# Six heads' share of half of the merge's latent blocks, moved into the attention

## The chip, the cores and the metric

The kernel runs on one core of one Trainium2 chip. The metric is device time in microseconds (us) of one execution; several executions are timed and their median is compared.

## The reference, cut to what matters

One decoder layer: a first feed-forward half-step, two token mixers side by side (softmax "latent" attention with 8 heads, called MLA, and stick-breaking attention with 8 heads, called SB), a gated merge of the two, a second feed-forward half-step and a gated embedding. The change touches the merge alone:

```python
g_mla, g_sb = jnp.split(jax.nn.sigmoid(gates), 2, axis=-1)
merged = g_mla * (o_mla @ w_branch_mla[i]) + g_sb * (o_sb @ w_branch_sb[i])
h = h + merged @ w_out[i]
```

`o_mla` and `o_sb` are 1024 tokens by 512 (8 heads of 64), the branch weights are 512 by 1024, `w_out` is 1024 by 1024. Every product is made of three TensorE products of split numbers (high by high, high by low, low by high), with float32 sums.

## The kernel before, in words

Activations lie channel by token. A weight is loaded by SP's queue into a buffer of the pool `raw` (three buffers of 512 KB, handed out in turn), split by ScalarE (high part) and GpSimd (low part) into a buffer of the pool `d` (six buffers), and used by TensorE (`load_split`, lines 133 to 144). The same three `raw` buffers also carry the gates, outputs and operands of the filling work below. TensorE's order is the order in which the code is written. The order on the other engines and on SP's queue is made by a scheduler from priorities and its own timing model, so it can differ from the written one.

The attention (from line 1097) goes through 48 units, 24 of SB and then 24 of MLA (8 heads with 3 units each). A unit goes in steps: transposes of probabilities, scores of the next unit, products with the values. After each step `fill(ns)` draws *filling work*, which is matmuls of a generator, until the step has taken 2500 ns (SB) or 1600 ns (MLA) of modelled TensorE time. In the SB half the filler is `gates()`. In the MLA half it is `branches_sb()`: for each of eight blocks of 128 channels (`ct`) the product of `o_sb` with the branch weight, times its gate, written to the scratch tensor `msb_d` in HBM. `left[0]` holds the nanoseconds of filler that remain; when it is used up, MLA's steps run without filling, save that the last head's last units empty the generator.

The merge (from line 1288) follows. `merge_up(ct, d)` computes block `ct` of `o_mla` times the branch weight (24 matmuls of 512 columns: two halves of tokens, four pairs of heads, three products), multiplies it by the gate, adds `msb_d` and splits the sum into `hid`. `chunked` (line 267) lays this beside the product with `w_out`: blocks 0, 1 and 2, then `down_chunk` on blocks 0 and 1 (96 matmuls), block 3, block 4, `down_chunk` on 2 and 3, and so on, each with its weight loads. Also at the start of the merge `h` (8 loads of 512 KB from `h_spill`, line 1297) and a gain row (`gbc`, line 209) are loaded.

Of the kernel before, what the change touches and what calls it, by code (L numbers as in the profile page):

```python
# [2 lines left out]

# [8 lines left out]
F32 = mybir.dt.float32  # L12
# [7 lines left out]
P = 128  # L20
# [3 lines left out]
KT = DM // P  # L24
# [22 lines left out]
def hybrid_layer_kernel(  # L47
# [42 lines left out]
    def bank():  # L90
        return pool_of["T"].tile([P, 512], F32, tag="T", name="T")
# [40 lines left out]
    def load_split(parts, n, home=None):  # L132

        raw = rawp.tile([P, 1024], F32, tag="raw", name="raw")
        for c0, src in parts:
            a, b = src.shape[1], src.shape[2]
            nc.sync.dma_start(out=raw[:, c0:c0 + a * b].rearrange("p (a b) -> p a b", a=a), in_=src)
        d = new_d() if home is None else home
        nc.scalar.copy(d[:, HI, :n], raw[:, :n])  # L139
        w = n // pieces[0]  # L140
        for c0 in range(0, n, w):
            c = slice(c0, c0 + w)
            nc.gpsimd.tensor_sub(d[:, LO, c], raw[:, c], d[:, HI, c].bitcast(F32))  # L143
        return d
# [45 lines left out]
    def mm3(ps, lh, ll, rh, rl, start, stop):  # L190
        mm(ps, lh, rh, start, False)
        mm(ps, lh, rl, False, False)
        mm(ps, ll, rh, False, stop)
# [73 lines left out]
    def chunked(h, n, up, wo, scale, ahead, order, after):  # L267

        load, compute = up

        def rows(f0):
            return [w_rows(wo, (f0 + j) * P, 0, 1024) for j in range(2)]

        d0, d1 = load(0), load(1)
        hids = [compute(0, d0), compute(1, d1)]
        for f in range(0, n - 4, 2):
            d0 = load(f + 2)
            dw = rows(f)
            d1 = load(f + 3)
            nxt = [compute(f + 2, d0)]  # L280
            for _ in down_chunk(h, hids, dw, scale):
                pass
            nxt.append(compute(f + 3, d1))
            hids = nxt
        d0, d1 = load(n - 2), load(n - 1)
        dw = rows(n - 4)
        hids.append(compute(n - 2, d0))
        dw += rows(n - 2)
        hids.append(compute(n - 1, d1))
        ahead()  # L290
        for t in down_chunk(h, hids, dw, scale, order):
            after(t)
# [487 lines left out]
    st_p.close()  # L780
    psum_pools(st_p, "2", 2)

    def branch_w(w, ct):
        d = load_split([(0, w[:, ct * P:(ct + 1) * P].rearrange("(k q) c -> q k c", q=P))], 512)
        return d[:, :, :512].rearrange("q l (k c) -> q l k c", k=4)

    def load_row(src, i):
        gt = rawp.tile([P, 1024], F32, tag="raw", name="gt")
        nc.sync.dma_start(out=gt, in_=src[i])
        return gt  # L790

    def branch_mm(ps, d, o, tk):
        for k in range(4):
            mm3(ps, d[:, HI, k], d[:, LO, k], o[HI][:, k, tk], o[LO][:, k, tk], k == 0, k == 3)


    def gates():
# [14 lines left out]
    def branches_sb(first):  # L812

        nxt = first
        for ct in range(KT):
            d = nxt
            if ct + 1 < KT:
                nxt = branch_w(w_branch_sb, ct + 1)
            gt = load_row(gate_d, KT + ct)
            bt = rawp.tile([P, 1024], F32, tag="raw", name="bt")  # L820
            for half in range(2):
                tk = slice(half * 512, (half + 1) * 512)
                ps = bank()
                for k in range(4):
                    mm3(ps, d[:, HI, k], d[:, LO, k], o_t[1][HI][:, k, tk], o_t[1][LO][:, k, tk], k == 0, k == 3)
                    yield
                nc.scalar.copy(bt[:, tk], ps)
                nc.gpsimd.tensor_mul(bt[:, tk], bt[:, tk], gt[:, tk])
            nc.sync.dma_start(out=msb_d[ct], in_=bt)

    filler = [gates()]
# [400 lines left out]
    def start_mla():  # L1232
        first = branch_w(w_branch_sb, 0)
        fill(1e9)
        for b in range(2):
            o_t.append([upool.tile([P, 4, S], F32R, tag="u", name="oT") for _ in range(2)])
        for j in range(4):
            split_o(o_t[1], j, pairs[j], slice(0, S))
        filler[0] = branches_sb(first)
        left[0] = KT * 24 * 216.0  # L1240
# [12 lines left out]
    for n, (m, hd, un) in enumerate(units):  # L1253
        if (m, hd, un) == (1, 0, 0):
            while queue:
                run_av()
            start_mla()
        todo = []
        if n + 1 < len(units):
            m2, hd2, un2 = units[n + 1]  # L1260
            todo = []
            for c in unit_ch[un2]:
                both = (2 * c, 2 * c + 1)
                todo += [(m2, hd2, ix) for ix in ([both] if m2 or c < 2 else [both[:1], both[1:]])]
        if un == 1:
            head_of(m, hd + 1) if hd + 1 < H else head_of(m + 1, 0) if m == 0 else None
        steps = []
        for c in unit_ch[un]:
            steps += av_steps(hd, c, [probs.pop((m, hd, 2 * c + a)) for a in range(2)], head_of(m, hd)[3], m == 1)
        for k, (tr, ac) in enumerate(steps):  # L1270
            t0 = pe["t"]
            take = -(-len(todo) // (len(steps) - k))
            pt = tr()
            for x_ in todo[:take]:
                scores(*x_)
            todo = todo[take:]
            queue.append((pt, ac))
            if len(queue) > 2:
                run_av()
            goal = (2500.0, 1600.0)[m]  # L1280
            if m == 0 or left[0] > 0 or (hd == H - 1 and un > 0):
                fill(t0 + goal - pe["t"])
# [17 lines left out]
    def merge_up(ct, d):  # L1300
        if ct % 2 == 0:
            if ct == 0:
                gmt[0] = [new_d(F32) for _ in range(2)]
            else:
                both = upool.tile([P, 2, 2, S], F32, tag="u", name="gm")
                gmt[0] = [both[:, b] for b in range(2)]
            for b, src in enumerate((gate_d, msb_d)):
                nc.sync.dma_start(out=gmt[0][b], in_=src[ct:ct + 2].rearrange("a q n -> q a n"))
        gt, mt = gmt[0][0][:, ct % 2], gmt[0][1][:, ct % 2]
        pool, bufs = (hid_a, 1) if ct % 4 == 3 else (hid_b, 3)  # L1310
        hid = pool.tile([P, 2, S], F32R, tag="hid", name="hid", bufs=bufs)
        for half in range(2):
            tk = slice(half * 512, (half + 1) * 512)
            ps = bank()
            branch_mm(ps, d, o_t[0], tk)
            m = mp.tile([P, 512], F32, tag="m", name="m", bufs=2)
            nc.vector.tensor_mul(m, ps, gt[:, tk])
            nc.vector.tensor_add(m, m, mt[:, tk])
            split_hidden(hid, tk, m)
        return hid  # L1320
# [12 lines left out]
    def after2(t):  # L1333
# [6 lines left out]
        else:  # L1340
# [3 lines left out]
            left.sums(t - 4, (0,) if t == 4 else (0, 1))  # L1344

    g2 = bcast_row(mp, ffn2_norm, DM)
    chunked(h, KT, (lambda ct: branch_w(w_branch_mla, ct), merge_up), w_out, 1.0, ahead,
            tuple(range(NT)), after2)
    need("a11")
    st.close()  # L1350
# [79 lines left out]
```

## Time and profile before

| what | us |
|---|---|
| median of 3 runs (2368.03 to 2371.63) | 2369.64 |
| the profiled execution's own time | 2370.18 |
| its span on the chip | 2368.3 |
| TensorE (PE) busy in the span | 2294.6 |
| VectorE (DVE) busy | 1525.6 |
| ScalarE (ACT) busy | 959.2 |
| GpSimd (POOL) busy | 847.7 |

The span runs from the first to the last instruction. Times in the rows count from its start. In this execution the filler `branches_sb` ends at about 1425 us, the attention's last value product at 1480 us, and the merge lies from there to about 1621 us.

### The profile page before, as it was taken

Reading aid. Unit: us, or ns where it says so; the run is one execution under the profiler, and the core shown is the slowest. Engines: PE = TensorE matmul, PEld = TensorE weight load, DVE = VectorE, ACT = ScalarE, POOL = GpSimd, SP = SyncE. Lnnn points to the kernel's source line nnn. Section 1 sums busy time; section 2 is a strip of 40 time slices with the busy share of each in tenths; the row PEclk is TensorE's granted clock in tenths of the full one; section 3 lists DMA queues with packets and bytes.
Section 4 is the critical chain, followed back from the end, with each engine's and each line's share of the span. In section 5 each row is a group of like instructions: output and inputs, shape, how many; then the busy total and the mean of one; then the engine's idle time right before and its main releaser. Section 6 shows DMA issues by size and latency. Waiting matters only on the chain.

```text
span 2368.3 us, 30098 instructions
## 1 busy us (share of the span) xinstructions
PE 2294.6 (97%) x11160; PEld 1913.8 (81%) x11160; DVE 1525.6 (64%) x1997; ACT 959.2 (41%) x1612; POOL 847.7 (36%) x650
## 2 busy tenths in 40 slices
PE   8899999999999999899999998998999999999999
PEld 7788888878888988777777887886888888888887
DVE  7667676567772325567777778557676666577842
ACT  5323233335352224456556666224332333244441
POOL 6544444400031233543333532547444444300030
PEclk9999999999999999999999999999999999999999
DMA  6223233395564334884443666512333332575442
GB/s 232 84 89 112 92 122 97 112 340 170 178 199 124 88 94 122 235 213 99 112 100 91 164 163 198 187 63 80 95 118 99 103 111 89 206 282 187 139 133 80
DMA packets 293890, 331.85 MB, mean 140 GB/s; under 512 B 16624, under 2 KB 200176, under 8 KB 293744
## 3 DMA queue, kind: packets, MB, share of 16 engines
q1 hardware_dynamic: 269808, 296.38, 39.2%
q0 software_dynamic: 23936, 33.56, 6.8%
q8 instruction: 87, 1.43, 0.2%
q14 instruction: 59, 0.48, 0.1%
HBM read 230.79 MB, written 99.09 MB: 139 GB/s over the span
## 4 chain that ended last, share of the span: by engine, by line
PE 78%; DVE 8%; DMA 6%; POOL 3%; issue 2%; ACT 2%; SPq 0%; DVEq 0%; ACTq 0%; POOLq 0%
PE T L183 37%; PE T L411 33%; PE A L183 5%; PE T L187 4%; DMA raw<-in_ffn_w_out_dram 2%; DVE D L1182 1%; POOL D L143 1%; DMA k_d<-ev 1%; DMA hv<-v_d 1%; POOL D L372 1%; DVE D L1183 1%; DVE p L1182 1%; DVE pt L214 0%; POOL hid L265 0%; DVE ts L390 0%
## 5 line engine op out<-in xcount | busy, mean ns | idle before, releaser
L411 PE MATMUL T<-u,D 128*128 128x512 f32 x3168 | 734.7, 391 | 11.6 <-DVE u L434 6.6
L411 PEld LDWEIGHTS T<-u,D 128*128 128x128 f32 x3168 | 596.9, 189 | 137.7 <-ACT p L419 5.3
L183 PE MATMUL T<-D 128*128 128x512 f32 x1944 | 451.0, 392 | 5.5 <-DVE u L214 2.1
L183 PEld LDWEIGHTS T<-D 128*128 128x128 f32 x1944 | 365.1, 189 | 82.5 <-ACT D L537 2.7
L372 POOL TENSOR_TENSOR D<-ts,D 128x1024 fp32r<-128x1024 f32 x88 | 215.9, 2454 | 299.5 <-ACT D L371 299.4
L183 PE MATMUL T<-u,D 128*128 128x512 f32 x1152 | 288.2, 396 | 11.1 <-DVE op L1132 11.1
L143 POOL TENSOR_TENSOR D<-raw,D 128x256 fp32r<-128x256 f32 (+6 forms) x159 | 188.0, 1207 | 295.1 <-ACT D L139 272.5
L183 PEld LDWEIGHTS T<-u,D 128*128 128x128 f32 x1152 | 209.2, 188 | 55.1 <-DVE op L1132 16.2
L537 ACT CAST D<-raw 128x512 fp32r<-128x512 f32 (+1 forms) x154 | 123.7, 807 | 223.8 <-PE T L183 109.2
L371 ACT CAST D<-ts 128x1024 fp32r<-128x1024 f32 x88 | 92.5, 1051 | 293.2 <-PE T L411 273.6
L183 PE MATMUL T<-D,u 128*128 128x512 f32 (+2 forms) x960 | 195.9, 362 | 0.0
L203 POOL TENSOR_SCALAR r<-ss 128x1 f32<-128x1 f32 (+2 forms) x52 | 16.2, 312 | 497.8 <-ACT un L223 403.3
L183 PEld LDWEIGHTS T<-D,u 128*128 128x128 f32 x960 | 166.1, 188 | 21.9
L538 DVE TENSOR_TENSOR D<-raw,D 128x512 fp32r<-128x512 f32 (+1 forms) x146 | 131.2, 901 | 59.6 <-ACT D L537 59.1
L214 DVE TENSOR_TENSOR pt<-T,pt 128x512 fp32r<-128x512 f32 (+1 forms) x160 | 101.2, 634 | 73.8 <-ACT pt L213 72.7
L372 POOL TENSOR_TENSOR D<-raw,D 128x1024 fp32r<-128x1024 f32 x44 | 120.3, 2734 | 33.1 <-ACT D L371 33.1
L411 PE MATMUL T<-u,wb 128*128 128x512 f32 x528 | 126.8, 389 | 0.0
L388 DVE TENSOR_TENSOR ts<-raw 128x512 f32<-128x512 f32 x44 | 36.8, 836 | 136.1 <-POOL D L372 131.4
L213 ACT CAST pt<-T 128x512 fp32r<-128x512 f32 (+1 forms) x160 | 86.7, 544 | 90.7 <-PE T L187 88.8
L411 PEld LDWEIGHTS T<-u,wb 128*128 128x128 f32 x528 | 99.1, 188 | 20.6
L454 DVE TENSOR_TENSOR hidf<-u,sg 128x512 f32<-128x512 f32 x44 | 105.4, 2395 | 9.8 <-ACT sg L452 9.4
L389 DVE TENSOR_TENSOR ts<-raw,ts 128x512 f32<-128x512 f32 x44 | 110.3, 2506 | 0.0
(227 smaller groups left out, 3320.1 us busy)
## 6 DMA issues: line engine op xcount, KB each, us to landing
raw<-in_ffn_w_in_dram SPq DMA_DIRECT2D x88, 512.0 KB, 4.0
raw<-hs_d SPq DMA_DIRECT2D x154, 256.0 KB, 2.8
hs_d<-hidf SPq DMA_DIRECT2D x110, 256.0 KB, 2.2
raw<-in_ffn_w_out_dram SPq DMA_DIRECT2D x110, 256.0 KB, 3.2
raw<-in_w_in_dram SPq DMA_DIRECT2D x28, 512.0 KB, 4.4
raw<-in_ffn_w_out_dram SPq DMA_DIRECT2D x22, 512.0 KB, 6.1
h_spill<-h SPq DMA_DIRECT2D x16, 512.0 KB, 3.1
gate_d<-gate SPq DMA_DIRECT2D x16, 512.0 KB, 3.0
```

The costliest lines, as they stand in the source:

```text
L143: nc.gpsimd.tensor_sub(d[:, LO, c], raw[:, c], d[:, HI, c].bitcast(F32))
L183: nc.tensor.matmul(ps, lhs, rhs, start=start, stop=stop)
L187: nc.tensor.transpose(ps, src, ident)
L213: nc.scalar.copy(hi, ps)
L214: nc.vector.tensor_sub(lo, ps, hi.bitcast(F32))
L371: nc.scalar.copy(d[:, HI], src)
L372: nc.gpsimd.tensor_sub(d[:, LO], src, d[:, HI].bitcast(F32))
L389: nc.vector.tensor_sub(ts[:, 1], b22, ts[:, 0])
L411: nc.tensor.matmul(ps, b[:, l, k], a[:, r, k], start=start and k == n == 0, stop=k == 3 and n == 2, skip_group_check=True)
L454: nc.vector.tensor_mul(t["hid"][:, 512:], u3, sg)
L537: nc.scalar.copy(d[:, HI, cols], src)
L538: eng.tensor_sub(d[:, LO, cols], src, d[:, HI, cols].bitcast(F32))
```

## The change

The work of blocks 2 to 5 in the merge is cut in two. For the first three pairs of heads, which are complete when unit (MLA, head 6, unit 1) begins, the product is made in the attention as filling work by a new generator `branches_mla`. It takes the gate and `msb_d`, adds up and writes the result back to `msb_d`. The merge then makes only the last pair of heads for these blocks (6 matmuls in place of 24), with a branch weight of 128 rows in place of 512.

```diff
-    def branch_w(w, ct):
-        d = load_split([(0, w[:, ct * P:(ct + 1) * P].rearrange("(k q) c -> q k c", q=P))], 512)
-        return d[:, :, :512].rearrange("q l (k c) -> q l k c", k=4)
+    def branch_w(w, ct, k0=0):
+        n = (4 - k0) * P
+        d = load_split([(0, w[k0 * P:, ct * P:(ct + 1) * P].rearrange("(k q) c -> q k c", q=P))], n)
+        return d[:, :, :n].rearrange("q l (k c) -> q l k c", c=P)
...
-    def branch_mm(ps, d, o, tk):
-        for k in range(4):
-            mm3(ps, d[:, HI, k], d[:, LO, k], o[HI][:, k, tk], o[LO][:, k, tk], k == 0, k == 3)
+    def branch_mm(ps, d, o, tk, k0=0):
+        for k in range(k0, 4):
+            mm3(ps, d[:, HI, k - k0], d[:, LO, k - k0], o[HI][:, k, tk], o[LO][:, k, tk], k == k0, k == 3)
...
+    EARLY = range(2, 6)
+
+    def branches_mla():
+
+        nxt = branch_w(w_branch_mla, EARLY[0])
+        for ct in EARLY:
+            d = nxt
+            if ct + 1 in EARLY:
+                nxt = branch_w(w_branch_mla, ct + 1)
+            bt = rawp.tile([P, 1024], F32, tag="raw", name="bt")
+            for half in range(2):
+                tk = slice(half * 512, (half + 1) * 512)
+                gm = rawp.tile([P, 2, 512], F32, tag="raw", name="gm")
+                for j, src in enumerate((gate_d, msb_d)):
+                    nc.sync.dma_start(out=gm[:, j], in_=src[ct, :, tk])
+                ps = bank()
+                for k in range(3):
+                    mm3(ps, d[:, HI, k], d[:, LO, k], o_t[0][HI][:, k, tk], o_t[0][LO][:, k, tk], k == 0, k == 2)
+                    yield
+                nc.scalar.copy(bt[:, tk], ps)
+                nc.gpsimd.tensor_mul(bt[:, tk], bt[:, tk], gm[:, 0])
+                nc.gpsimd.tensor_add(bt[:, tk], bt[:, tk], gm[:, 1])
+            nc.sync.dma_start(out=msb_d[ct], in_=bt)
...
+        if (m, hd, un) == (1, 6, 1):
+            filler[0] = itertools.chain(filler[0], branches_mla())
+            left[0] += len(EARLY) * 18 * 216.0
...
-            branch_mm(ps, d, o_t[0], tk)
+            branch_mm(ps, d, o_t[0], tk, 3 if ct in EARLY else 0)
...
-    chunked(h, KT, (lambda ct: branch_w(w_branch_mla, ct), merge_up), w_out, 1.0, ahead,
+    chunked(h, KT, (lambda ct: branch_w(w_branch_mla, ct, 3 if ct in EARLY else 0), merge_up), w_out, 1.0, ahead,
```

In the changed file every line behind the first is one lower, and behind the new generator 26 to 29 lower (L183 becomes L184, L1297 becomes L1326).

TensorE, the end of the attention and the start of the merge (`T<-ident,D` are transposes, `T<-pt,hv` value products, `T<-oT,D` branch products). Before:

```order
L187 MATMUL T<-ident,D 128x128 x4
L183 MATMUL T<-pt,hv 128x256 x4
L187 MATMUL T<-ident,D 128x128 x3
L183 MATMUL T<-pt,hv 128x256 x10
L183 MATMUL T<-pt,hv 128x128 x2
L183 MATMUL T<-oT,D 128x512 x72
L183 MATMUL T<-D,hid 128x512 x96
L183 MATMUL T<-oT,D 128x512 x48
```

and with the change:

```order
L188 MATMUL T<-ident,D 128x128 x4
L184 MATMUL T<-pt,hv 128x256 x4
L184 MATMUL T<-oT,D 128x512 x6
L188 MATMUL T<-ident,D 128x128 x3
L184 MATMUL T<-pt,hv 128x256 x4
L184 MATMUL T<-oT,D 128x512 x6
L184 MATMUL T<-pt,hv 128x256 x6
L184 MATMUL T<-pt,hv 128x128 x2
L184 MATMUL T<-oT,D 128x512 x54
L184 MATMUL T<-D,hid 128x512 x96
L184 MATMUL T<-oT,D 128x512 x12
```

Twelve groups of six branch matmuls stand between the steps of heads 6 and 7, the last one just ahead of the attention's last value products, and the merge's groups shrink from 72 and 48 to 54 and 12.

SP's queue from the last of the filling work to the merge's loads (`bt` is a block's result, `gm` with 512 columns a half's gate and `msb_d`; blocks 0, 1 and 2 are the first three loads of `w_branch_mla` before, `raw_13057`, `raw_13062` and `raw_13145` with the change). Before:

```order
L829 DMA msb_d_142<-bt_12131 128x1024
L137 DMA raw_12894<-in_w_branch_mla_dram 128x4x128
L137 DMA raw_12977<-in_w_branch_mla_dram 128x4x128
L1308 DMA D_12899<-gate_d_141 128x2x1024
L1308 DMA D_12900<-msb_d_142 128x2x1024
L137 DMA raw_12982<-in_w_out_dram 128x1024
L137 DMA raw_12987<-in_w_out_dram 128x1024
L137 DMA raw_12992<-in_w_branch_mla_dram 128x4x128
L137 DMA raw_13202<-in_w_branch_mla_dram 128x4x128
L1297 DMA h2_12878<-h_spill_134 128x1024 x8
```

and with the change:

```order
L855 DMA msb_d_142<-bt_12882 128x1024
L847 DMA gm_12987<-gate_d_141 128x512
L847 DMA gm_12987<-msb_d_142 128x512
L138 DMA raw_13057<-in_w_branch_mla_dram 128x4x128
L1326 DMA h2_13046<-h_spill_134 128x1024 x3
L855 DMA msb_d_142<-bt_12957 128x1024
L1326 DMA h2_13046<-h_spill_134 128x1024 x5
L210 DMA gbc_13055<-in_ffn2_norm_dram 128x1024
L138 DMA raw_13062<-in_w_branch_mla_dram 128x4x128
L138 DMA raw_13145<-in_w_branch_mla_dram 128x128
L138 DMA raw_13150<-in_w_out_dram 128x1024
L1337 DMA gm_13354<-msb_d_142 128x2x1024
```

The weights of blocks 0 and 1, the first gates and both first rows of `w_out` stood ahead of the eight loads of `h`; with the change the weight of block 0 stands behind the last operands of the filling work, and the rest behind the eight loads, the last write of the filling work and the gain row. The rest goes on with the gates of blocks 0 and 1 and the second row of `w_out`.

GpSimd at the same place, with the change (`L853` and `L854` are the new product and sum, `L1166` a split of an attention output, `L144` the low part of a weight):

```order
L854 TENSOR_TENSOR bt_12957<-bt_12957,gm_12958 128x512
L853 TENSOR_TENSOR bt_12957<-bt_12957,gm_12987 128x512
L1166 TENSOR_TENSOR oT_10647<-op_12482,oT_10646 128x256
L854 TENSOR_TENSOR bt_12957<-bt_12957,gm_12987 128x512
L144 TENSOR_TENSOR D_13059<-raw_13057,D_13059 128x512
L144 TENSOR_TENSOR D_13064<-raw_13062,D_13064 128x512
```

The low part of the weight of block 0 now comes behind the last operations of the filling work.

## Rows read from the trace of the kernel before

**Rows 1.** Busy time by stretch: PE, PEld, DVE, ACT, POOL, then PEclk, DMA share, GB/s.
```profile
1470.00:1480.00 10.00, 7.47 (x48) 6.87 (x48) 7.68 (x13) 7.82 (x16) 5.60 (x5) 0.83 0.42 134
...
1490.00:1500.00 10.00, 10.00 (x46) 8.29 (x45) 6.66 (x9) 3.73 (x6) 8.72 (x7) 1.00 1.02 397
1500.00:1520.00 20.00, 20.00 (x90) 16.57 (x89) 10.03 (x15) 3.35 (x4) 7.39 (x5) 1.00 0.14 41
```
**Rows 2.** Timeline of PE, 1405 to 1485 us: start, us, what, idle before.
```profile
1405.71 1.60 PE L183 MATMUL T<-oT,D 128*128 128x512 f32 x6
1407.16 0.49 PE L187 MATMUL T<-ident,D 128*128 128x128 f32 x3
...
1407.96 1.54 PE L183 MATMUL T<-oT,D 128*128 128x512 f32 x6
...
1452.30 0.33 PE L187 MATMUL T<-ident,D 128*128 128x128 f32 x1 [0.57 <-DVE pt L214]
1453.25 0.55 PE L187 MATMUL T<-ident,D 128*128 128x128 f32 x3 [0.62 <-DVE D L1206]
...
1464.66 0.33 PE L187 MATMUL T<-ident,D 128*128 128x128 f32 x1 [0.40 <-DVE pt L214]
1465.57 0.55 PE L187 MATMUL T<-ident,D 128*128 128x128 f32 x3 [0.57 <-DVE D L1206]
...
1472.74 0.33 PE L187 MATMUL T<-ident,D 128*128 128x128 f32 x1 [1.63 <-DVE pt L214]
1473.83 0.55 PE L187 MATMUL T<-ident,D 128*128 128x128 f32 x3 [0.75 <-DVE D L1206]
...
1478.31 2.02 PE L183 MATMUL T<-pt,hv 128*128 128x256 f32 x12
1480.16 5.00 PE L183 MATMUL T<-oT,D 128*128 128x512 f32 x21
```
**Rows 3.** Timeline of SP's queue: start, us, what it issues.
```profile
1428.70 14.92 SPq L137 DMA_DIRECT2D raw<-in_w_branch_mla_dram  x2
...
1483.25 5.08 SPq L1297 DMA_DIRECT2D h<-h_spill  x8
1488.38 0.44 SPq L209 DMA_DIRECT2D gbc<-in_ffn_norm_dram  x1
```
**Rows 4.** The tile bt, 1200 to 1500 us: engine, op, min/median/max ns; landing of its writes.
```profile
L827 ACT COPY bt<-T x16: 578/585/586, 1303.2 to 1426.0; 128x512 f32<-128x512 f32 x16
L828 POOL TENSOR_TENSOR bt<-bt,gt x16: 1272/1282/1292, 1303.9 to 1426.9; 128x512 f32<-128x512 f32 x16
...
DMA to landing us min/median/max: 2.8/3.6/15.0
```
**Rows 5.** DMA issues from 1250 to 1600 us: count, KB, median us to landing.
```profile
raw<-in_w_branch_mla_dram SPq DMA_DIRECT2D x8, 256.0 KB, 3.5
```
**Rows 6.** Timeline of POOL, around the attention's end.
```profile
1482.49 0.73 POOL L1140 TENSOR_TENSOR oT<-op,oT 128x256 fp32r<-128x256 f32 x1
```
**Rows 7.** Groups of POOL by form, 1480 to 1600 us: busy, mean ns.
```profile
L143 POOL TENSOR_TENSOR D<-raw,D 128x1024 fp32r<-128x1024 f32 x8 | 19.6, 2453 | 19.5 <-ACT D L139 19.5
L143 POOL TENSOR_TENSOR D<-raw,D 128x512 fp32r<-128x512 f32 x5 | 6.8, 1380 | 11.4 <-ACT D L139 11.4
```
**Rows 8.** DMA issues from 1479 to 1500 us: count, KB, median us to landing.
```profile
gbc<-in_ffn_norm_dram SPq DMA_DIRECT2D x1, 512.0 KB, 10.9
```
**Rows 9.** Timeline of PE around its longest wait in the second feed-forward's start.
```profile
1618.10 2.98 PE L411 MATMUL T<-u,D 128*128 128x512 f32 x12
...
1632.18 2.04 PE L187 MATMUL T<-ident,s 128*128 128x128 f32 x8 [10.22 <-DVE u L214]
1633.88 3.64 PE L411 MATMUL T<-u,D 128*128 128x512 f32 x12
```
**Rows 10.** The tile m in the merge: durations of its operations, min/median/max ns.
```profile
L1317 DVE TENSOR_TENSOR m<-T,gm x12: 678/692/692, 1494.1 to 1569.3; 128x512 f32<-128x512 f32 x12
L1318 DVE TENSOR_TENSOR m<-m,gm x12: 693/1426/2282, 1494.8 to 1570.0; 128x512 f32<-128x512 f32 x12
```

More of the change, by code (lines that the diff above doesn't have):

```diff
@@ L1 @@
+import itertools
 import math
```

## The prediction

> **What bounds the kernel now.** I read four views in this order: the busy times by stretch, the timeline of PE at the end of the attention, the timeline of SP's queue at the same place, and the durations of what the change adds. The first shows that the merge runs with PE busy without a break, 90 matmuls of 512 columns in 20 us, so 0.222 us each [rows 1]. There, work taken from PE is time gained, as long as the weights and gates arrive. The end of the attention is different: PE is busy 7.47 of 10 us between 1470 and 1480, and its granted clock is 0.83 [rows 1]. The steps without filling work wait for a chain through VectorE, and the timeline shows those waits one by one [rows 2]. The third view shows why the merge starts at 1480.16 us without a wait: the weights of blocks 0 and 1 were issued from 1428.70 on, and the eight loads of h, 4 MB, start at 1483.25, behind everything that the first blocks need [rows 3].
>
> **The change, part by part.**
>
> *Twelve groups of six matmuls go into the attention.* A group took 1.45 us when the SB filler had one (from 1405.71 to 1407.16) [rows 2]; twelve are 17.4 us. By the order they stand just ahead of five of the waits or pairs of waits that remain: of 0.57 and 0.62, 0.40 and 0.57, 1.63 and 0.75 us [rows 2], together 4.5 us, and they fill these; at the other places they hide nothing. The clock of 0.83 over 10 us [rows 1] means 3.4 us at 1.2 instead of 2.4 GHz, a loss of 1.7 us, which goes when PE has no gap there. The attention ends 17.4 - 4.5 - 1.7 = 11.2 us later.
>
> *The merge loses 72 matmuls*, 72 x 0.222 = 16.0 us. If all else stayed covered the change would gain 16.0 - 11.2 = 4.8 us. The remaining parts are about that cover.
>
> *The filling work now ends together with the attention, in three buffers.* Call E the moment at which the last value product ends. The SB filler's last write was issued before 1428.70 [rows 3], 50 us ahead of the merge. The new filler's last group stands in the order just ahead of the last value products, and every block of it needs four tiles (a weight, two halves' operands, a result) of the three `raw` buffers. So the loads wait for each other. From block 4's last matmul to E there are three groups of 1.45 us, three steps of transposes and value products (one took 0.80 us, from 1407.16 to 1407.96 [rows 2]) and the last products, 1.85 us (1478.31 to 1480.16 [rows 2], part of it at the low clock; I take 1.0): 7.8 us. At E - 7.8 the copy of block 4's second half starts, 0.59 us, then product and sum on GpSimd, 1.28 us each [rows 4] (the sum is taken as long as the product, whose form it has), and one split of 0.73 us that stands between them [rows 6]: E - 3.9. The write lands after 2.8 to 3.6 us [rows 4]: E - 1.1 to E - 0.3. Only then can the operands of block 5's second half be loaded into that buffer: two loads of 256 KB, of which one alone lands in 3.5 us [rows 5], the second 0.6 us behind it at the 397 GB/s of rows 1: E + 3.0 to E + 3.8. Then product, split and sum again, 3.3 us, and behind these in GpSimd's order the low part of block 0's weight, 1.38 us [rows 7], which was loaded meanwhile: E + 7.7 to E + 8.5. **First wait of PE: 8 us.** It is between nothing (if GpSimd were not behind) and 12.
>
> *SP's queue.* With the change the eight loads of h stand ahead of block 1's weight. They waited for GpSimd's last split: it ended at 1483.22 [rows 6], the first load was issued at 1483.25 [rows 3]. With the change this split stands between product and sum, at about E + 5.4. From the first load's issue to the landing of the gain row behind them it took 1488.38 + 10.9 - 1483.25 = 16.0 us [rows 3, 8]; this is nine transfers of 512 KB with few others between them. So the gain row lands at E + 21.4, block 1's weight (256 KB) 0.7 us later, its split takes 0.6 (as a copy of that width, [rows 4]) and 1.4 us [rows 7]: the high part is there at E + 22.7, the low one at E + 24.1. PE has only block 0 meanwhile, 24 x 0.222 = 5.3 us, until E + 13.4. **Second wait: 10 us**; nothing, if this weight overtook the loads of h, up to 14 if the last write of the filling work is slow (it stands in the queue too, and the slowest such write landed after 15.0 us [rows 4]).
>
> *Gates and rows of w_out.* PE makes blocks 1 and 2, 30 matmuls, until E + 30.7. Behind block 1's weight stand 64 KB, a row of w_out and three transfers of 1 MB (gates and `msb_d`), together 3.7 MB or 9.2 us at 397 GB/s: E + 31.3. Then two VectorE operations (0.69 us each at best [rows 10]), cast and subtraction make `hid`, and the second row of w_out, which got its buffer only at E + 24, lands 1.3 us behind the gates and is split by GpSimd in 2.45 us [rows 7] behind the subtractions: E + 38.5. The 96 matmuls of the first `down_chunk` can start slowly at E + 35 and run freely from E + 38.5. **Third wait: 8 us**, between 2 and 12.
>
> *The clock.* After PE's wait of 10.22 us twelve matmuls took 3.64 us instead of 2.98, and the eight transposes behind the wait 2.04 [rows 9]. I take 1 us for each of two long waits, 2 us together (0 to 5). *Less cover later:* block 4 is now 6 matmuls, 1.3 us, between block 3 and the `down_chunk` that needs it, while a half's way through VectorE, ScalarE and GpSimd takes some 3.3 us: 1 us (0 to 5).
>
> **Sum**: 11.2 - 16.0 + 8 + 10 + 8 + 2 + 1 = +24.2 us. The profiled execution took 2370.2 us, so it becomes 2394.4; it stood 0.5 us above the median of the runs, so I predict 2394 for the median.
>
> **A rule against the change.** VectorE and GpSimd slow each other here: an addition with two inputs from SBUF took 0.69 to 2.28 us where GpSimd worked beside it, while the product with one input from PSUM stayed at 0.69 [rows 10]. The change puts sixteen products and sums on GpSimd beside the scaling of the probabilities (L1206), for which PE waits [rows 2]. The Trainium skill, "SBUF — State Buffer", section "Who interferes with whom", says that VectorE and GpSimd share a pair of ports that one of them holds for a whole instruction, so the other blocks fully; the trace agrees for the addition, and by that rule each scaling that PE waits for could be late by one GpSimd operation. In this sum the groups of 1.45 us cover it; it gives a rival below.
>
> **Rivals.**
> *It works as written* (chance 0.06): the weights and gates are there at E, only the first two parts count, 2370.2 - 4.8 - 0.5 = 2365, faster. For it speaks that the DMA engines are idle much of the time around (0.14 of their time from 1500 to 1520 [rows 1]). Against it stands the order of SP's queue. The point that decides is whether block 1's weight lands before E + 5.3.
> *The merge is covered, but the two engines block each other* (0.04): three GpSimd operations of 1.28 us land on the path of the probabilities, 3.8 us, and 2369, no change. Against it: the groups stand ahead of most of those waits.
> *The weight of block 1 overtakes the loads of h* (0.13): the second wait goes, the first and third stay: 2394 - 10 = 2384.
> *The chain through the buffers is slower still* (0.09): each of the write and load steps near its slow end, first wait 12, second 14, third 10: 2394 + 10 = 2404. For it: that landings stretch to 15.0 us [rows 4].
> The change does what it says: the twelve groups are in the order, and the merge's groups shrink, so nothing is left for a case without effect.
>
> **How the numbers follow.** The forecast has 0.68. The range reaches down over the overtaking weight with the clock's and the later waits' terms left out, to 2378, and up to the slow chain, 2406; it leaves out the cases without the waits. About 0.2% is what a measurement of this kernel can tell from no change. Faster is the case as written, 0.06; the same 0.04; slower the rest, 0.90.
>
> **What would show it.** In the timeline of PE, waits of several us right behind the attention's last value products (for ScalarE's and GpSimd's splits of a weight), a second one after 24 branch matmuls, a third at the first `w_out` products. On SP's timeline the loads of h ahead of block 1's weight and that weight landing over 10 us after the merge begins. The attention's last product should come some 11 us later. The forecast is wrong if the merge starts without a wait, or if the waits are there and the time is not longer. If they are there, but short, the terms of the chain were too large.

## The result: slower by 35 us

The changed kernel took 2405.02 us (median of 4 runs, 2403.32 to 2409.61), the kernel before 2369.69 beside it: a ratio of 1.015, interval 1.0137 to 1.0163. The prediction was 2394 with a range of 2378 to 2406. The direction and the places are right, and the time lies inside the range, but 11 us above the forecast.

### The profile after

The timeline of PE from the attention's end through the merge. Times are from the start of the span, 2403.6 us long; E, the end of the last value product, is at 1490.1.

```profile
1489.00 1.06 PE L184 MATMUL T<-pt,hv 128*128 128x256 f32 x8
1495.55 1.22 PE L184 MATMUL T<-oT,D 128*128 128x512 f32 x2 [5.48 <-ACT D L140]
1497.61 7.86 PE L184 MATMUL T<-oT,D 128*128 128x512 f32 x22 [0.85 <-POOL D L144]
1514.71 9.95 PE L184 MATMUL T<-oT,D 128*128 128x512 f32 x30 [9.24 <-ACT D L140]
...
1525.83 0.50 PE L184 MATMUL T<-D,hid 128*128 128x512 f32 x1 [0.64 <-POOL hid L266]
1528.26 0.49 PE L184 MATMUL T<-D,hid 128*128 128x512 f32 x1 [1.93 <-ACT hid L265]
1529.82 0.49 PE L184 MATMUL T<-D,hid 128*128 128x512 f32 x1 [1.06 <-POOL D L144]
1532.31 23.27 PE L184 MATMUL T<-D,hid 128*128 128x512 f32 x91 [2.00 <-POOL hid L266]
...
1561.21 20.91 PE L184 MATMUL T<-D,hid 128*128 128x512 f32 x91 [1.43 <-POOL hid L266]
1581.96 12.40 PE L184 MATMUL T<-oT,D 128*128 128x512 f32 x54
...
1597.72 0.50 PE L184 MATMUL T<-D,hid 128*128 128x512 f32 x1 [1.55 <-POOL hid L266]
1600.21 1.22 PE L184 MATMUL T<-D,hid 128*128 128x512 f32 x2 [1.99 <-ACT hid L265]
1603.39 15.84 PE L184 MATMUL T<-D,hid 128*128 128x512 f32 x57 [1.96 <-POOL hid L266]
```

Where [rows 2] go on without a wait at 1480.16, there are three groups of waits here: 6.3 us (5.48 + 0.85) for block 0's weight, 9.24 for block 1's, and 5.6 at the first products with `w_out` (0.64, 1.93, 1.06, 2.00). A fourth, 1.43 and then 1.55, 1.99 and 1.96, comes later, at the second pair of blocks and at the last `down_chunk`, which takes blocks 4 to 7 together (192 products). The kernel before has one wait of 0.63 us at that place:

```profile
1570.57 13.22 PE L183 MATMUL T<-D,hid 128*128 128x512 f32 x57 [0.63 <-POOL hid L265]
```

The queue of SP there shows the three buffers and the loads of `h` in their order; [rows 3] had block 1's weight at 1428.70, ahead of `h`.

```profile
1487.89 0.32 SPq L855 DMA_DIRECT2D msb_d<-bt  x1
1490.52 0.32 SPq L847 DMA_DIRECT2D gm<-gate_d  x1
1490.89 0.43 SPq L847 DMA_DIRECT2D gm<-msb_d  x1
1491.48 0.38 SPq L138 DMA_DIRECT2D raw<-in_w_branch_mla_dram  x1
1495.13 1.27 SPq L1326 DMA_DIRECT2D h<-h_spill  x3
1496.51 0.37 SPq L855 DMA_DIRECT2D msb_d<-bt  x1
1496.92 2.74 SPq L1326 DMA_DIRECT2D h<-h_spill  x5
1500.44 0.33 SPq L210 DMA_DIRECT2D gbc<-in_ffn_norm_dram  x1
1503.13 1.66 SPq L138 DMA_DIRECT2D raw<-in_w_branch_mla_dram  x2
```

Block 4's write is issued 2.2 us ahead of E, and 2.6 us later block 5's second operands follow into its buffer, then block 0's weight. GpSimd's timeline shows the rest of that chain: the product (L853) waits for those operands, the split of the last head's output (L1166) stands between product and sum, and the low part of block 0's weight (L144) behind them. It ends at 1497.56, E + 7.5.

```profile
1493.16 1.26 POOL L853 TENSOR_TENSOR bt<-bt,gm 128x512 f32<-128x512 f32 x1 [1.97 <-DMA gm<-gate_d]
1494.38 0.72 POOL L1166 TENSOR_TENSOR oT<-op,oT 128x256 fp32r<-128x256 f32 x1
1495.06 1.27 POOL L854 TENSOR_TENSOR bt<-bt,gm 128x512 f32<-128x512 f32 x1
1496.29 1.27 POOL L144 TENSOR_TENSOR D<-raw,D 128x512 fp32r<-128x512 f32 x1
```

Block 1's weight is issued at 1503.13. The issues from 1502 to 1510 us (KB, median us to landing) show that it took 10.9 us, against 3.5 in [rows 5]; the second row in the same view is the gates behind it.

```profile
raw<-in_w_branch_mla_dram SPq DMA_DIRECT2D x1, 256.0 KB, 10.9
D<-gate_d SPq DMA_DIRECT2D x1, 1024.0 KB, 10.9
```

The clock, in four stretches of the changed kernel (columns as in [rows 1]; the first number is PE's busy time in the stretch):

```profile
1493.00:1503.20 10.20, 6.81 (x15) 4.93 (x16) 0.00 (x0) 0.62 (x1) 4.39 (x4) 0.50 0.72 239
1510.00:1520.30 10.30, 5.47 (x12) 3.88 (x13) 0.00 (x0) 1.86 (x3) 4.05 (x3) 0.50 1.04 414
1530.50:1537.30 6.80, 4.99 (x12) 3.92 (x13) 4.94 (x6) 3.38 (x5) 6.17 (x6) 0.50 0.51 164
1598.80:1609.00 10.20, 6.83 (x15) 4.94 (x16) 4.07 (x4) 1.24 (x2) 5.77 (x4) 0.50 0.00 0
```

In each of the four groups of waits the granted clock fell from 1.00 to 0.50 (1.2 instead of 2.4 GHz) and stayed there for 6.8 to 10.3 us, which takes in the end of the wait and the matmuls behind it; 15 matmuls took 6.8 us, 0.45 each, where [rows 1] have 0.222.

**Where the 35 us are.** By span (2403.6 against 2368.3) they add up: the attention, from the start of its first filling matmul to the start of its last value product, is 192.4 us long instead of 180.7, +11.7; from there to the start of the second feed-forward's first product (at 1613.7 us in the kernel before, which ends the merge) it is 159.4 instead of 133.7, +25.7, although 16.0 us of matmuls are gone; the program ahead of the attention's MLA half was 1.9 us shorter in this execution, which is within what executions of one kernel differ by (6.3 us between the four runs).

### The profile page after: what moved, and what is told of

It reads as the page before. It is cut to its first block, busy times and chain, and to the rows that moved or that the text cites. A ratio compares the mean times of both kernels' runs of the same rounds, so it can differ in the third digit from the quotient of the medians.

```text
span 2403.6 us, 30194 instructions
## 1 busy us (share of the span) xinstructions
PE 2302.7 (96%) x11160; PEld 1914.0 (80%) x11160; DVE 1526.9 (64%) x1997; ACT 964.5 (40%) x1624; POOL 873.3 (36%) x682
## 3 DMA queue, kind: packets, MB, share of 16 engines
q8 instruction: 87, 1.43, 0.2%
## 4 chain that ended last, share of the span: by engine, by line
PE 76%; DVE 8%; DMA 6%; POOL 4%; issue 3%; ACT 2%; SPq 0%; DVEq 0%; ACTq 0%; POOLq 0%
PE T L184 35%; PE T L412 32%; PE A L184 5%; PE T L188 3%; DMA raw<-in_ffn_w_out_dram 2%; POOL D L144 2%; DVE D L1208 1%; DMA k_d<-ev 1%; POOL hid L266 1%; DVE D L1209 1%; DVE p L1208 1%; POOL D L373 1%; DMA h<-h_spill 1%; DMA D<-msb_d 1%; DVE pt L215 0%
## 5 line engine op out<-in xcount | busy, mean ns | idle before, releaser
L184 PE MATMUL T<-D 128*128 128x512 f32 x1944 | 448.7, 391 | 5.8 <-DVE u L215 2.3
L184 PEld LDWEIGHTS T<-D 128*128 128x128 f32 x1944 | 363.1, 188 | 82.8 <-DVE u L215 2.8
L373 POOL TENSOR_TENSOR D<-ts,D 128x1024 fp32r<-128x1024 f32 x88 | 215.8, 2454 | 300.3 <-ACT D L372 298.1
L144 POOL TENSOR_TENSOR D<-raw,D 128x256 fp32r<-128x256 f32 (+6 forms) x175 | 193.5, 1131 | 311.2 <-ACT D L140 288.1
L184 PE MATMUL T<-u,D 128*128 128x512 f32 x1152 | 288.0, 395 | 11.1 <-DVE op L1158 11.1
L184 PEld LDWEIGHTS T<-u,D 128*128 128x128 f32 x1152 | 209.2, 188 | 55.0 <-DVE op L1158 16.2
L184 PE MATMUL T<-D,u 128*128 128x512 f32 (+2 forms) x960 | 195.9, 362 | 0.0
L184 PEld LDWEIGHTS T<-D,u 128*128 128x128 f32 x960 | 166.1, 188 | 21.9
L373 POOL TENSOR_TENSOR D<-raw,D 128x1024 fp32r<-128x1024 f32 x44 | 120.4, 2735 | 32.9 <-ACT D L372 32.9
L184 PE MATMUL T<-oT,D 128*128 128x512 f32 x384 | 104.4, 414 | 16.7 <-ACT D L140 15.2
```

Source lines behind the costliest of these rows:

```text
L184: nc.tensor.matmul(ps, lhs, rhs, start=start, stop=stop)
L373: nc.gpsimd.tensor_sub(d[:, LO], src, d[:, HI].bitcast(F32))
```

## The experiments

Theory: the three waits at the start come from the shared buffers and from SP's queue, by the chain of the prediction. Rivals: the clock makes most of it; or the thinner cover later; or the filling in the attention itself.

**1. The filler gets a buffer of its own.**

```diff
+        work = upool.tile([P, 4, S], F32, tag="u", name="work")
...
-            bt = rawp.tile([P, 1024], F32, tag="raw", name="bt")
+            bt = work[:, ct % 2]
...
-                gm = rawp.tile([P, 2, 512], F32, tag="raw", name="gm")
+                gm = work[:, 2 + half].rearrange("q (j c) -> q j c", j=2)
```

> The filling work keeps its operands and results in one free 16 KB-per-partition buffer of pool u instead of the three raw buffers; raw then carries weights only, and SP's queue has the weights of blocks 0 and 1 ahead of the end of the attention and the loads of h behind the first gates and rows of w_out. Buffers and queue order as the cause: the three waits of PE at the start of the merge (5.5 and 0.9, 9.2, 5.6 us) and most of the half-clock time go, 2372 us (2364 to 2378). If the merge's short groups of 6 matmuls are the cause (a way through VectorE, ScalarE and GpSimd no longer covered): the waits at the w_out products stay, 2390 or more. If the filling work's operations on GpSimd hold up the attention: the attention's end stays late and the time is 2385 or more.

2379.48 us, ratio 1.0043 (1.0028 to 1.0058): 25 of the 35 us are gone, 1.5 us more than the range allowed remain. PE's waits from 1488 to 1600 us (total, times, longest):

```profile
PE T L184 <- POOL hid L266: 5.8, 4, 2.0
PE T L184 <- ACT hid L265: 2.0, 1, 2.0
PE T L184 <- POOL oT L1167: 0.6, 1, 0.6
```

No wait for a weight is left. The late waits stayed at 1.43, 1.55, 1.99 and 1.96, with 6.8 us of half clock behind them. The attention is 13.0 us longer than before, and the merge 4.5 us shorter instead of 16.0. What keeps the merge from its 16.0 us now is mostly the late cover, and it is no small term.

**2. The loads of h behind the second row of w_out; the buffers shared as in the change.**

```diff
-    for t in range(NT):
-        nc.sync.dma_start(out=h[:, t, :], in_=h_spill[t * P:(t + 1) * P, :])
...
+        if ct == 2:
+            load_h()
```

> The changed kernel with the eight loads of h queued on SP behind the second row of w_out of the first pair of blocks; all else stays, the buffers too. Queue order as the cause of the second wait: block 1's weight lands some 3 to 4 us behind the last write of the filling work, the wait of 9.2 us falls to 0 to 2 us, the first wait of 5.5 us stays, the half-clock time shrinks; 2392 us (2387 to 2397). If that weight is late because its buffer comes free late: the wait stays above 6 us and the time within 4 us of 2405.

2393.75 us, 1.0105 (1.0085 to 1.0125), as expected. All 54 branch matmuls run behind one wait:

```profile
1496.22 14.79 PE L184 MATMUL T<-oT,D 128*128 128x512 f32 x54 [6.03 <-ACT D L140]
```

So the second wait is the queue's order. The first stays, as it should if the shared buffers make it; experiment 1, which gives them up, takes it away. The third group of waits hardly changed (6.0 instead of 5.6 us).

**3 and 4. Only the merge's part; only the attention's part.** In the first no filling is done, so the first six heads' part of four blocks is missing from its output; in the second the filling's results go to scratch that nothing reads, and the merge makes these blocks whole (the second diff).

```diff
-            filler[0] = itertools.chain(filler[0], branches_mla())
-            left[0] += len(EARLY) * 18 * 216.0
+            pass
```
```diff
-            nc.sync.dma_start(out=msb_d[ct], in_=bt)
+            nc.sync.dma_start(out=spare_d[ct], in_=bt)
...
-            branch_mm(ps, d, o_t[0], tk, 3 if ct in EARLY else 0)
+            branch_mm(ps, d, o_t[0], tk, 0)
```

> No filling work at all, but the merge as in the change: blocks 2 to 5 take the last pair of heads alone, so the first six heads' part of four blocks is left out of the output. Buffers and queue order as the cause: the merge starts without a wait as before the change, loses 16.0 us of matmuls and keeps only the waits that the short groups make (1.4 at the second pair, 5.5 at the last): 2361 us (2356 to 2365). If the short groups are the cause of the slowdown: several waits of over 5 us stay in the merge, 2370 or more.

2363.96 us, 0.9978 (0.9969 to 0.9987), as expected. 72 matmuls less make the merge 6.6 us shorter, not 16.0. The timeline of PE there, at the last `down_chunk`, and GpSimd's under it:

```profile
1542.12 12.40 PE L184 MATMUL T<-oT,D 128*128 128x512 f32 x54
1554.36 1.97 PE L184 MATMUL T<-D,hid 128*128 128x512 f32 x8
1557.88 0.50 PE L184 MATMUL T<-D,hid 128*128 128x512 f32 x1 [1.54 <-POOL hid L266]
1560.37 1.14 PE L184 MATMUL T<-D,hid 128*128 128x512 f32 x2 [1.99 <-ACT hid L265]
1563.56 6.82 PE L184 MATMUL T<-D,hid 128*128 128x512 f32 x21 [2.04 <-POOL hid L266]
```
```profile
1542.82 8.03 POOL L144 TENSOR_TENSOR D<-raw,D 128x1024 fp32r<-128x1024 f32 x3 [13.49 <-ACT D L140]
1550.80 2.55 POOL L266 TENSOR_TENSOR hid<-m,hid 128x512 fp32r<-128x512 f32 x2
1553.30 2.85 POOL L373 TENSOR_TENSOR D<-raw,D 128x1024 fp32r<-128x1024 f32 x1
1556.12 2.94 POOL L266 TENSOR_TENSOR hid<-m,hid 128x512 fp32r<-128x512 f32 x2
1559.02 2.82 POOL L373 TENSOR_TENSOR D<-raw,D 128x1024 fp32r<-128x1024 f32 x1
1561.79 2.94 POOL L266 TENSOR_TENSOR hid<-m,hid 128x512 fp32r<-128x512 f32 x2
```

From 1542.82 to 1564.73 GpSimd has no gap: three splits of rows of `w_out`, two of the next feed-forward's weights (L373) and six subtractions of `hid`, 21.9 us. PE has 54 branch matmuls there (12.4 us) where it had 72 (16.5 us), so each `hid` is late. VectorE stands in the same chain: in the changed kernel its product for a half waited 3.56 and 1.16 us for GpSimd's subtractions (`m` has two buffers), and its additions (L1347) took 1.0 to 2.9 us beside GpSimd's work, where one without such company took 0.7.

```profile
1591.96 0.69 DVE L1346 TENSOR_TENSOR m<-T,gm 128x512 f32<-128x512 f32 x1 [3.56 <-POOL hid L266]
```

> The filling work of the change, with its results written to a scratch tensor that nothing reads, and the merge whole as before (24 matmuls per block): no work is saved. Filling work as the cause of the start's waits (buffers and queue order): attention 11.7 us later, the first w_out products run freely some 42 us behind the attention's end instead of 16, half-clock time there, no waits of the late merge: 2410 us (2403 to 2416). If the short groups make the start's waits: these go, and only the later end of the attention stays, 2382 us.

2402.78 us, 1.0137 (1.0122 to 1.0153), just below the range: with the merge whole, the filling alone costs 33 us, and no late wait over 0.7 us appears at the last `down_chunk`. The start's waits are 4.53, 0.71, 9.18 and 1.54 us; the last one is short, and PE has 48 matmuls instead of 30 ahead of the first `w_out` product there.

**5. Half of it: blocks 2 and 3 alone, with a buffer of their own as in experiment 1.**

```diff
-    EARLY = range(2, 6)
+    EARLY = range(2, 4)
```

> The change for two blocks (2 and 3) instead of four: six groups of six matmuls, the last one some 20 us ahead of the attention's end. Buffers and queue order as the cause: the raw buffers are free in time, the weights, gates and rows stand ahead of h on SP's queue, no long wait at the start of the merge; attention 8.7 - 2.2 = 6.5 us later, merge 8.0 us less matmul time, 2370 us (2365 to 2374). If the cost grows with the work moved (GpSimd, short groups): about half of the 35 us, 2387.

2368.95 us, 0.9996 (0.9987 to 1.0006), as expected: the attention is 7.0 us longer, the merge 8.2 shorter, with a single wait of 0.62 us in it.

**6. PE kept busy in the first two waits,** so that its clock stays up: 60 transposes ahead of block 0, 90 ahead of block 1, added to the changed kernel.

```diff
+    keep_busy(60)
...
+        if ct == 1:
+            keep_busy(90)
```

> The changed kernel with 60 transposes that nothing reads ahead of block 0 and 90 ahead of block 1 (about 5.5 and 8.5 us of PE work in the place of the waits). Loads as what sets the start: the products with w_out still run freely at the same place, some 42 us behind the attention's end; what the half clock adds behind it goes (2.9 us at the first 91 products): 2401 us (2397 to 2404). If the clock is the larger part of the loss: 2395 us or less.

2408.91 us, 1.0161 (1.0147 to 1.0175): a miss. The clock was indeed 1.00 through both blocks, and 22 of block 0's matmuls took 5.26 us instead of 7.86, 28 of block 1's and 2's 6.65. But the first free run of `w_out` products stands at E + 42.5, against E + 42.2 in the change:

```profile
1503.72 5.26 PE L184 MATMUL T<-oT,D 128*128 128x512 f32 x22 [1.66 <-POOL D L144]
1508.83 9.99 PE L1332 MATMUL T<-ident 128*128 128x128 f32 x90
...
1520.08 6.65 PE L184 MATMUL T<-oT,D 128*128 128x512 f32 x28 [0.62 <-POOL D L144]
1529.66 0.50 PE L184 MATMUL T<-D,hid 128*128 128x512 f32 x1 [2.93 <-ACT hid L265]
```

What the faster matmuls gave came back as a wait of 2.93 us for the gates' `hid`. (The 4 us above the change lie ahead of the merge: the MLA filling begins at 1302.0 instead of 1297.4 us in the two profiles.) The start is set by the loads; the half clock there costs nothing by itself. Behind the third waits, which the transposes don't fill, it stayed: 91 products in 22.99 us instead of 20.9, which the expectation had as gone.

**7. Three blocks, 0, 2 and 3** with the same buffer.

```diff
-    EARLY = range(2, 6)
+    EARLY = (0, 2, 3)
```

> Own buffer of pool u, and blocks 0, 2 and 3 in place of 2 to 5: nine groups of six matmuls, the last blocks of the merge whole. The theory: attention 9 x 1.45 - 4.5 - 1.7 + 1 = 7.9 us later, merge 12.0 us shorter, no long wait anywhere: 2365 us (2362 to 2369). If any moved block costs more than it saves: 2372 or more.

2370.46 us, 1.0001 (0.9993 to 1.001): a miss. The attention is 8.6 us longer, the merge only 8.0 shorter instead of 12: with 6 matmuls of block 0, waits of 0.66, 1.02, 0.31 and 1.07 us appear at its start, the first two for the last head's output.

**8. GpSimd relieved at the last `down_chunk`:** experiment 1 with the low parts of the next feed-forward's first two weights (L373) computed by VectorE.

```diff
-        up.load_a(0)
-        up.load_a(1)
+        up.load_a(0, eng=nc.vector)
+        up.load_a(1, eng=nc.vector)
```

> Own buffer of pool u, blocks 2 to 5, and the low parts of the second feed-forward's first two weights made by VectorE instead of GpSimd. GpSimd's queue as the cause of the late waits (three splits of w_out rows, two of these weights and the subtractions in one chain of 22 us under 12 us of matmuls): the waits of 1.6, 2.0 and 2.0 us at the last w_out products shrink to 1 us or less together, and the half clock behind them goes, 2373 us (2369 to 2377). If it is the way of one block through three engines: the waits stay, 2379.

2376.87 us, 1.0028 (1.0016 to 1.0039), at the range's upper end. The waits of 1.55 and 1.96 became 1.05 and 0.84, the half clock behind them 3.4 us instead of 6.8 (another 3.4 us stood at the second pair, where experiment 1 had none); the one for ScalarE's `hid`, 1.99, stayed. GpSimd's queue is thus part of the late waits; that the way of each half through VectorE, ScalarE and GpSimd makes the rest is argued, not shown. The interval overlaps that of experiment 1, so the gain is read from these waits and not from the two medians.

**9 and 10. The groups placed into PE's waits by a table,** for blocks 2 and 3, and for block 2 alone, both with a buffer of their own.

```diff
+    DRAWS = {(6, 1, -1): 2, (7, 0, -1): 2, (7, 1, -1): 4, (7, 2, -4): 2, (7, 2, -3): 1, (7, 2, -2): 1}
...
+            if m and (hd, un) >= (6, 1):
+                for _ in range(DRAWS.get((hd, un, k - len(steps)), 0)):
+                    next(filler[0], None)
```

An entry names head, unit and step (-1 is the unit's last) and how many groups of three matmuls are drawn there; the planner's own filling is off from head 6, unit 1 on. For block 2 alone the table is `{(6, 1, -1): 1, (7, 0, -1): 1, (7, 1, -1): 4}`.

> Two blocks (2 and 3) with a buffer of their own, and their twelve groups of three matmuls put by a table instead of by the planner's goal: two groups ahead of the last unit of head 6, two ahead of the second and four ahead of the third unit of head 7, four between the steps of that last unit. Theory (matmuls in the attention cost their own time except where they stand in one of PE's waits): 36 matmuls at 0.24 us are 8.7 us; they stand in the waits of 0.57 and 0.62, 0.40 and 0.57, 1.63 and 0.75 us, 4.5 us together, and in the 1.7 us that the half clock costs in the last unit, so the attention ends 2.5 us later; the merge is 8.2 us shorter, as with the two blocks that the planner placed. About 2364 us (2360 to 2368), beside 2369.6 of the kernel before. Rival (the filling delays ScalarE and GpSimd, so that the waits only move): no difference from the two blocks placed by the planner, 2369 us (2367 to 2371).

> One block (2) alone, with a buffer of its own, its six groups of three matmuls put by the same table: one group ahead of the last unit of head 6, one ahead of the second and four ahead of the third unit of head 7. Theory (only matmuls inside a wait are free): 18 matmuls at 0.24 us are 4.4 us against 3.8 us of waits that they can fill and 1.7 us of half clock, so the attention ends about 1 us sooner; the merge is 4.0 us shorter (18 matmuls of 0.222 us), all cover there kept. About 2365 us (2361 to 2368). Rival (the waits move behind the filling): the attention is 2 to 4 us longer and the time is that of the kernel before, 2369 us (2367 to 2371).

2369.57 us, 0.9996 (0.9988 to 1.0005), and 2369.28 us, 1.0 (0.9991 to 1.0009): both rivals held. The waits were not filled; they moved one place ahead, onto the filling or the value products. With two blocks:

```profile
1450.56 1.65 PE L184 MATMUL T<-oT,D 128*128 128x512 f32 x6 [0.83 <-DVE pt L215]
...
1474.03 0.74 PE L184 MATMUL T<-pt,hv 128*128 128x256 f32 x4 [2.03 <-DVE pt L215]
1474.61 2.90 PE L184 MATMUL T<-oT,D 128*128 128x512 f32 x12
```

Both wait for VectorE's evacuation of transposes. The pool `T` has four PSUM banks in this phase, handed out in turn, and the filling takes one of them: its bank would be the one that the next step's transposes waited for [rows 2]. The trace doesn't name banks, so this is inferred here; the next two experiments test it.

**11 and 12. The same blocks, each half's nine matmuls together and ahead of the step's value products** (a fourth draw evacuates the half). Two things change at once, the place and the grouping.

```diff
+    DRAWS = {(6, 1, -1): 4, (7, 0, -1): 4, (7, 1, -1): 4, (7, 2, -3): 4}
...
+            if m and (hd, un) >= (6, 1):
+                for _ in range(DRAWS.get((hd, un, k - len(steps)), 0)):
+                    next(filler[0], None)
             if len(queue) > 2:
                 run_av()
```

For block 2 alone the table is `{(7, 0, -1): 4, (7, 1, -1): 4}`.

> Two blocks (2 and 3) as in the run before, but each half's nine matmuls together, and drawn in the last step of a unit ahead of its value products instead of behind them: one half each in the last unit but one of head 6, the first and second unit of head 7, and one inside the third. In the run with the groups behind the value products, the filling's output took the next of four rotating PSUM banks and waited itself for VectorE's evacuation (0.83, 0.94, 2.03 us). Theory (the bank of a filling that stands a place earlier is free, so it runs inside the wait): waits of 1.19, 0.97 and 2.38 us shrink to under 0.5 each and the half clock in the last unit goes; 36 matmuls of 0.24 us, 8.7, less 4.0 and 1.7 make the attention 3 us longer, the merge is 8.2 shorter: 2365 us (2361 to 2368). Rival (the wait is VectorE's, and the filling's own work on ScalarE and GpSimd pushes it out): waits remain 3 us and more, 2369 us (2367 to 2372).

> One block (2) with its two halves of nine matmuls ahead of the value products of the last step of the first and of the second unit of head 7. Theory (it runs inside the wait): 18 matmuls, 4.3 us, stand in waits of 0.97 and 2.38 us and in the 1.7 us that the half clock costs; the attention keeps its length within 1 us, the merge is 4 us shorter: 2366 us (2363 to 2368). Rival (the waits stay as long behind the filling): attention 4 us longer, 2369.5 us (2368 to 2372).

2364.77 us, 0.9977 (0.9969 to 0.9986), and 2366.59 us, 0.9983 (0.9974 to 0.9992): the theory held in both. With two blocks:

```profile
1448.68 2.33 PE L184 MATMUL T<-oT,D 128*128 128x512 f32 x9
...
1452.00 0.65 PE L188 MATMUL T<-ident,D 128*128 128x128 f32 x4 [0.51 <-ACT work L855]
...
1473.33 0.66 PE L188 MATMUL T<-ident,D 128*128 128x128 f32 x4 [0.31 <-ACT work L855]
```

Of the 4.5 us of waits in [rows 2] 1.2 are left (0.51 and 0.31 for the copy of the filling's own bank, which shows that the transposes behind it reuse that bank, and 0.33 at 1479.57 for VectorE). The granted clock from 1470 to 1480 us is 1.00, where [rows 1] have 0.83; in experiment 9 it was 1.00 as well, so it isn't what sets the two apart:

```profile
1470.00:1480.00 10.00, 9.35 (x59) 7.82 (x58) 7.24 (x11) 7.51 (x17) 8.35 (x8) 1.00 0.99 383
```

The attention is 2.9 us longer, the merge 8.2 shorter; with one block the attention is as long as before and the merge 4.1 shorter. Whether the place or the grouping does it was not tried apart. This version, two blocks, is 0.2% faster than the kernel before and 1.7% faster than the change.

## Why the prediction was right, and what it mis-sized

- *The attention ends 11.2 us later.* Measured 11.7. That the attention hides about a third of the 17.4 us of matmuls and no more was right. Of the 4.5 us of waits that the groups were to fill (the working counts five places and lists three, six waits in all) 1.2 stayed, as 0.44, 0.33 and 0.45; the granted clock from 1470 to 1480 us was 1.00, as forecast.
- *The merge loses 16.0 us.* Right as work; but the merge became only 6.6 us shorter even with nothing else changed (experiment 3).
- *First wait, 8 us.* Measured 6.3, with two matmuls in between. The chain is the predicted one: write, operands, product and sum, the low part of block 0's weight, which ended at E + 7.5 where E + 7.7 to 8.5 was forecast. Experiment 1 takes it away.
- *Second wait, 10 us.* Measured 9.2. The weight stood behind eight loads of `h` and landed 10.9 us after its issue; its high part was there at E + 24.6, against E + 22.7. Experiment 2 takes it away by the queue's order alone.
- *Third wait, 8 us.* Measured 5.6, in four pieces, but the free run starts at E + 42.2, not E + 38.5: 3.7 us of the miss. The last of the gates' transfers landed at E + 32.9 where the gates were forecast for E + 31.3, late as everything behind `h`; the rest of the 3.7 us lies behind it, in the `hid` chain and the splits of the rows of `w_out` (waits of 1.93, 1.06 and 2.00 us). The half clock at blocks 1 and 2 (30 matmuls in 9.95 us) is no cause: experiment 6 removes it and the free run does not move.
- *Less cover later, 1 us (0 to 5).* **This is the term that was mis-sized most**: 6.9 us of waits (1.43, 1.55, 1.99 and 1.96). The step "block 4 is now 6 matmuls, while a half's way takes some 3.3 us" looked at one pair with GpSimd free. At the last `down_chunk` GpSimd has 21.9 us of work in one piece, and 54 matmuls don't cover it.
- *The clock, 2 us (0 to 5).* Too small: 91 products took 23.27 instead of 20.9 us behind the third waits and the last 57 15.84 instead of 13.2 behind the late ones, 5.0 us together.

The miss of 11 us is thus about 3.7 of the chain, 5.9 of late cover, 3.0 of the clock and 0.5 of the attention, less 1.9 that the part ahead of it was shorter.

That the time lies inside the range is in part luck. The three waits at the start were forecast at 26 us and measured 21.1; the free run still came 3.7 us later, as part of what was forecast as waiting went into matmuls at the low clock (54 in 19.0 us instead of 12.0). The late cover went beyond its own bounds (0 to 5 us) and the clock reached the top of its own; the range holds them only because its upper end was taken from the slow chain, which did not happen.

Of the rivals, the case as written and the overtaking weight are excluded by the timeline. Two engines blocking each other showed no extra price in the attention, which ended where the sum has it: from 1425 us on, no scaling of the probabilities took longer than 0.94 us in the changed kernel, where one of 896 columns took 1.74 us beside GpSimd before the change. In the late `hid` chain they do meet (experiment 3), and the prediction had no term for it there. The slow chain, at 2404 with a chance of 0.09, hit the time, but by another mechanism: the first two waits were shorter than forecast, not longer.

## What to carry to other kernels

Work moved under another engine's waits isn't free by itself: look where it stands in its engine's order and whether it takes something, such as a PSUM bank in a rotation, that the waiting step needs. Here the same 36 matmuls gave nothing in threes behind the value products and 0.2% in nines ahead of them. Before filling work is extended up to a phase's end, follow its buffers and its queue into the next phase: a load that was issued 50 us early and is now issued late queues behind all that the next phase starts with. And matmuls taken from a phase were also cover for the other engines' work; sum that work over each block group and compare it with what PE has left.

## What was unexpected

At the late waits the low clock outlasts by far the waits that come before it. At the last `down_chunk` of the change it fell within a wait of 1.99 us that followed one of 1.55, and stayed at 0.50 for 10.2 us; with 1.54, 1.99 and 2.04 us in experiment 3 it stayed for 6.8. The Trainium skill, "TensorE: Matmul & The Clock Gate", section "HAM oscillation — how this bites in real kernels", describes a kernel that waits for a DMA before each short burst of matmuls and starts every burst at the low clock; the trace agrees for the two weights, and shows the same where GpSimd and ScalarE are waited for. And a low clock inside a stretch that loads bound costs nothing: experiment 6 kept it full there and gained nothing.
